# Five places of work in a hybrid decoder layer: row sums' low parts, first halves' transposes, one residual, the last pair's window parts and one token quarter's load

## The chip, the cores and the metric

The kernel runs on one core of one Trainium2 chip. Its time is the device time of one execution in microseconds (us). The core has five engines with a program of their own each: TensorE (PE, matrix products and transposes), VectorE (DVE), ScalarE (ACT), GpSimd (POOL) and SyncE (SP, which here only starts DMA transfers, as POOL and ACT also do). Each engine takes its instructions in order, so an instruction that waits holds up all that stand behind it on its engine. PE's loads of the stationary operand have rows of their own (PEld).

## What is computed

One step of a layer with three head groups, for 4096 prompt tokens and 64 sample tokens, in fp32 with a model width of 1024:

```
h = rmsnorm(x, g_pre);  z = h @ w_in                       # 1024 -> 10 column groups
conv, gate:   out_a = silu(cg) * cb * conv3(cc * ch)       # 256 channels
window:       out_b = silu(ag) * window_attention(q, k, v) # 8 heads of 64, 2 kv heads, window 128, a sink per head
memory:       out_c = silu(mg) * memory_attention(mq)      # 4 heads, 256 memory tokens
y = concat(out_a, out_b, out_c) @ w_out                    # 1024 -> 1024
x = x + rmsnorm(y, g_post)
```

Outputs are the new x of both token groups, and the last keys, values and convolution inputs.

## The kernel before

**Numbers.** Operands of PE are pairs of fp32r parts: a high part `hi` (a cast on ACT, line 358, or 1676 in the pairs) and a low part `lo`, the difference, on DVE (line 359, or 1679). A product is three matmuls: hi x hi, lo x hi, hi x lo.

**Input projection.** It runs in three phases of the output columns (`ph` 0, 1, 2; the first is phase one in the change's title). The 4160 tokens form eight blocks of 520, and each block's product with the weights is a Strassen-Winograd form of seven products `p` over halves of tokens, inputs and columns, so that the tokens of a block are quarters: B11 and B12, B21 and B22. `T1` to `T4` (`x_5T`, `hi_5T`, ...) are differences of quarters. A quarter is loaded to a tile of its own (`x_6B`: a quarter of block 6) or into the shared tiles `place`, scaled on ACT (line 326), and split (358, 359). In the first phase, `next_block` (line 545) says at which product of a block the quarters of the next one are loaded, by SP's queue, and scaled. In the same phase the token rows `nat` are loaded for the norms' sums of squares (ACT line 276), and in blocks 3 to 6 four weight tiles `ws..A` are loaded and summed on DVE (lines 201 to 207) for later phases. The products are PE line 368.

**Attention and output projection.** 4096 tokens are sixteen chunks of 256, each with two halves `h` (odd and even). A half goes through three steps, called between product steps of the output projection: `first_half` (window scores `ws`, the products of the half before, gates, window softmax), `memory_half` (memory scores `xs`) and `second_half`, where `window_turns` transposes the softmaxed window scores `sm` on PE (line 1376, `wt`); ACT copies them (1305, `wpt`), POOL masks them into `wpv` and `wpt` (1310, 1313), and PE reads these in line 1388. For the memory heads, DVE takes the maximum (`xmx`, `xnm`), ACT the exponentials (1178, `xp`), DVE reciprocals of the sums (`xrd`, 1184), POOL scales (1190), PE transposes (1366, `xt`), and ACT copies (1367).

**Output projection.** Its first three chunk pairs are six plain blocks of 128 tokens (`Block.run`, line 1618: two column halves p of eight steps k); a block ends with a norm: DVE `yn` (1645), ACT squares (1646), POOL `yst` (1653), and a residual `xr` (DVE 1658, with its store), which `finish_block` takes from the list `left` at step (0, 5) of the next block. Between them sit the weight sums `wsum..`, `wt..` (1836 to 1848) that the pairs need. From chunk 3 on, `Pair.run` (line 1686) computes two blocks at once in a seven-product form, whose operands are `pa` (plain parts), `pr` (row sums), `pw` (window parts), `pd` (diagonal sum) and `pc` (column differences), and whose accumulators are `y_c`. There are thirty positions `e` in a pair; a table says which piece of another step is called at which position.

**What sets the order.** PE's order is the order of the code. In the first phase the other engines also run in written order; in attention, the other engines' order is set by a scheduler from priorities and dependences, except where `keep_in_program_order` pins it. So the positions of the table move instructions of all engines. These are the lines:

```python
memory_at = {...} | turn_of(16, 27)
second_at = {h: n + (12 if h == 2 else 9 if h == 8 else 8) for h, n in first_at.items()} | turn_of(18, 32)
...
at(e - 10, p.plain_parts)
at(e - 3, p.row_sums)
...
at(e + 4, lambda p=p: p.window_parts(0))
at(e + 7, lambda p=p: p.window_parts(1))
```

Of the kernel before, what the change touches and what calls it, by code (L numbers as in the profile page):

```python
# [52 lines left out]
def hybrid_layer(ctx: ExitStack, tc: tile.TileContext, a: dict):  # L53
# [491 lines left out]
    def next_block(ph, b, p):  # L545
# [5 lines left out]
        if nph < 2:  # L551
            jobs += {0: "B11", 3: "B21 B12", 4: "B22"} .get(p, "").split() if ph == 0 else \
                    {0: "B11", 3: "B21", 4: "B12", 5: "B22"}.get(p, "").split()
            jobs = [load(o) for o in jobs]
# [1024 lines left out]
    class Block:  # L1579
# [38 lines left out]
        def run(self, starts):  # L1618
# [5 lines left out]
            for p in range(2):  # L1624
                cs = slice(512 * p, 512 * p + 512)
                acc = psum("z", f"y{b}_{p}")
                for k in range(KT):
                    starts.get((p, k), lambda: None)()
                    if m < P:
                        l, w = self.terms[p][k]  # L1630
                        for r in range(2):
                            TE.matmul(acc, l, w[:, r], start=k + r == 0, stop=k + r == KT)
                        continue
                    if (p, k) == (0, 5):
                        finish_block()
                    for i, (l, r) in enumerate(((0, 0), (1, 0), (0, 1))):
                        TE.matmul(acc, self.hl[l][:, k], wo[k][p][:, r], start=k + i == 0, stop=k + i == KT + 1)  # L1637
# [25 lines left out]
    class Pair:  # L1663
# [24 lines left out]
        def sums_of(self, raw, t, *terms):  # L1688
# [5 lines left out]
            return lambda pinned=False: self.lows(t, raw, pinned)  # L1694

        def row_sums(self):
            t = self.parts("pr")
            self.rows = [t[:, :, 0:2], t[:, :, 2:4]]
            raw = sums["sum"].tile([P, 512], F32, tag="sum", name=f"sum{self.c}")
            self.sums_of(raw, t, *((self.mix(slice(2, 4), n), self.mix(slice(0, 2), n), ALU.add) for n in range(2)))()  # L1700

# [19 lines left out]
        def run(self, starts, sample=lambda: None):  # L1721
# [70 lines left out]
            if not last:  # L1792
# [3 lines left out]
                product(c22, self.w[1], plain(1, range(4, 8)), False)  # L1796
                added(1, 1, c22)
                scaled(1, 1)
                ends(1)
# [122 lines left out]
    memory_at = {h: n + (7 if h == 2 else 3 if h == 8 else 3) for h, n in first_at.items()} | turn_of(16, 27)  # L1922
    second_at = {h: n + (12 if h == 2 else 9 if h == 8 else 8) for h, n in first_at.items()} | turn_of(18, 32)
    first_at |= turn_of(12, 24)

    what, pending = {}, []
    between = []

# [19 lines left out]
    for c, p in pairs.items():  # L1948
# [7 lines left out]
        at(e + 6, lambda: left.pop(0)(True) if left else None)  # L1956
        at(e + 7, lambda p=p: p.window_parts(1))
        at(e + (7 if c == NCH - 1 else 9), p.diagonal_sum)
# [151 lines left out]
```

## Time and profile before

| | |
|---|---|
| time, median of 3 runs | 1528.67 us (1528.08 to 1529.4) |
| profiled execution, its own time | 1541.16 us |
| its span | 1539.4 us |
| mean granted TensorE clock | 0.996 |
| TensorE, VectorE, ScalarE, GpSimd busy | 98%, 78%, 55%, 25% |
| data moved by DMA | 319.71 MB, mean 208 GB/s |

The span counts from the first to the last instruction of the profiled execution. A row of the timeline reads: start in us, duration in us, engine, line, operation, output <- inputs, sizes, count, and in brackets how long the engine stood idle before it and for whom. Rows that follow one another with the same line and operation are joined. The table of waits gives, for each instruction and the one that it waited for, total us, number and longest. The granted clock in a window is a share of full speed.

### The profile page before, as it was taken

What the parts mean: (1) busy time and instruction counts of PE and PEld (TensorE: products, weight loads), DVE (VectorE), ACT (ScalarE), POOL (GpSimd) and SP (SyncE); (2) the same over time, 40 slices, a digit from 0 to 9 for tenths busy, and PEclk for the clock granted to TensorE, in tenths of its full rate; (3) what the DMA queues carried; (4) which work ended last, traced back from release to release, by engine and by line L of the source; (5) the groups of instructions that cost most, each with busy time, mean ns of one, the idle gap of its engine ahead of it and who ended that gap; (6) DMA issues with size and microseconds to landing.
All of it is one profiled execution on the core that took longest, in us unless ns stands there. A gap on an engine that the chain in (4) does not pass through costs nothing.

```text
span 1539.4 us, 30947 instructions
## 1 busy us (share of the span) xinstructions
PE 1510.8 (98%) x11497; PEld 1386.8 (90%) x11497; DVE 1208.1 (78%) x2089; ACT 843.1 (55%) x2066; POOL 391.5 (25%) x576
## 2 busy tenths in 40 slices
PE   9999999999999999999999999999999999999997
PEld 9999999999999999999999999777788778777875
DVE  6779876899988777896777768876877888888864
ACT  6676655565422222354454536665666666666652
POOL 0222322211300000000111301234455444454631
PEclk9999999999999999999999999999999999999999
DMA  9989999878855333478787698998755555666552
GB/s 261 170 241 217 285 288 260 244 255 290 223 182 180 114 123 125 165 234 288 225 269 239 208 305 246 282 234 222 200 165 155 158 165 160 172 172 165 152 196 69
DMA packets 217322, 319.71 MB, mean 208 GB/s; under 512 B 37397, under 2 KB 143381, under 8 KB 217141
## 3 DMA queue, kind: packets, MB, share of 16 engines
q1 hardware_dynamic: 196837, 273.54, 60.5%
q0 software_dynamic: 19616, 43.15, 10.5%
q8 instruction: 91, 1.49, 0.4%
q10 hardware_dynamic: 720, 1.05, 0.2%
q14 instruction: 58, 0.48, 0.1%
HBM read 208.50 MB, written 110.15 MB: 207 GB/s over the span
## 4 chain that ended last, share of the span: by engine, by line
PE 68%; DVE 12%; issue 4%; DMA 4%; ACT 3%; POOL 1%; SPq 1%; DVEq 0%; ACTq 0%; POOLq 0%
PE c L368 49%; PE y_c L1737 9%; PE y L1637 2%; DVE sm L1295 2%; DVE sm L1341 1%; PE xt L1366 1%; DVE xr L1658 1%; DMA kst<-qd 1%; PE ws L1331 1%; DVE xmx L1169 1%; ACT sm L1287 1%; DMA nat<-in_x_p 1%; DVE wmx L1279 1%; PE mem_acc L790 1%; DMA zs<-in_w_out 1%
## 5 line engine op out<-in xcount | busy, mean ns | idle before, releaser
L375 DVE TENSOR_TENSOR z<-c,z 128x520 f32<-128x520 f32 (+1 forms) x308 | 194.3, 644 | 82.2 <-PE c L368 81.3
L1737 PE MATMUL y_c<-wo,pw 128*128 128x512 f32 (+1 forms) x636 | 158.4, 391 | 0.5 <-DVE yn L1775 0.5
L1287 ACT ACTIVATE sm<-sm,wnm 128x128 f32<-128x128 f32 x256 | 99.4, 389 | 72.0 <-DVE wnm L1281 72.0
L1737 PEld LDWEIGHTS y_c<-wo,pw 128*128 128x128 f32 x636 | 114.1, 188 | 27.2 <-issue 5.4
L1190 POOL TENSOR_SCALAR xp<-xp,xrd 128x256 f32<-128x256 f32 x128 | 67.6, 548 | 80.0 <-DVE xrd L1184 75.5
L1178 ACT ACTIVATE xp<-xs,xnm 128x256 f32<-128x256 f32 x128 | 59.0, 473 | 24.6 <-DVE xnm L1170 24.1
L737 POOL CAST wmask<-negs 128x256 uint8<-128x256 f32 x1 | 1.2, 1213 | 270.0 <-DMA negs<-in_wmask 270.0
L1313 POOL TENSOR_SCALAR_AFFINE_SELECT wpt<-wpt 128x512 f32<-128x512 f32 x64 | 59.0, 934 | 39.8 <-ACT wpt L1305 37.9
L1310 POOL TENSOR_SCALAR_AFFINE_SELECT wpv<-wpt 128x512 f32<-128x512 f32 x62 | 51.8, 848 | 58.5 <-ACT wpt L1305 58.4
L1637 PE MATMUL y<-wo,mh 128*128 128x512 f32 x192 | 64.5, 398 | 0.2 <-ACT y L1646 0.2
L276 ACT ACTIVATE nat<-nat 104x1024 f32<-104x1024 f32 x40 | 42.3, 1057 | 35.2 <-DMA nat<-in_x_p 35.2
L1331 PE MATMUL ws<-kst,q 128*128 128x256 f32 (+1 forms) x480 | 55.7, 297 | 0.0
L1341 DVE COPY_PREDICATED sm<-wmask,ws 128x512 f32<-128x512 uint8 x60 | 40.5, 729 | 18.5 <-ACT sm L1340 18.5
L1658 DVE SCALAR_TENSOR_TENSOR xr<-yn,yst,xr 128x1024 f32<-128x1024 f32 (+2 forms) x35 | 52.4, 1501 | 3.1 <-POOL yst L1653 3.0
L407 ACT CAST zh<-z 128x520 fp32r<-128x520 f32 x56 | 33.3, 624 | 36.5 <-DVE z L375 31.9
L377 ACT COPY z<-c 128x520 f32<-128x520 f32 (+1 forms) x44 | 24.4, 554 | 51.2 <-PE c L368 47.0
L1331 PEld LDWEIGHTS ws<-kst,q 128*128 128x128 f32 (+1 forms) x480 | 46.4, 187 | 4.1
L1287 ACT ACTIVATION_READ_ACCUMULATOR sm<-sm,wnm 128x1 f32 x256 | 47.9, 187 | 0.0
L1295 DVE TENSOR_TENSOR sm<-sm,wrd 128x512 f32<-128x512 f32 x64 | 44.8, 700 | 1.1
L164 POOL DMA_DIRECT2D md<-th x48 | 26.3, 548 | 75.6 <-DVE th L425 61.3
L1367 ACT COPY xp<-xt 128x1024 f32<-128x1024 f32 x30 | 30.4, 1014 | 27.1 <-POOL wpv L1310 16.1
L1737 PE MATMUL y_c<-wtT,pa 128*128 128x512 f32 x156 | 41.1, 400 | 3.8 <-DVE yn L1755 3.8
(1035 smaller groups left out, 5563.5 us busy)
## 6 DMA issues: line engine op xcount, KB each, us to landing
q<-qd SPq DMA_DIRECT2D x168, 128.0 KB
xr<-in_x_p SPq DMA_DIRECT2D x32, 512.0 KB
nat<-in_x_p SPq DMA_DIRECT2D x39, 416.0 KB
o_yp<-xr SPq DMA_DIRECT2D x31, 512.0 KB
kst<-qd SPq DMA_DIRECT2D x112, 128.0 KB
md<-th POOLq DMA_DIRECT2D x48, 260.0 KB, 7.3
qd<-zh SPq DMA_DIRECT2D x48, 260.0 KB
qd<-z SPq DMA_DIRECT2D x48, 260.0 KB
```

Of the source, the lines that this page charges most:

```text
L368: TE.matmul(bank[:, :HW], l, r, start=first and i == 0, stop=last and i == 3 * KH - 1)
L375: add = lambda dst, other: V.tensor_tensor(dst, c, other, op=ALU.add)
L1178: S.activation(p[:, i, :], s[:, i, :], AF.Exp, bias=nm[:, i : i + 1], scale=SCALE, accum_out=den[:, i : i + 1])
L1190: G.tensor_scalar(p[:, i, :], p[:, i, :], self.rds[h][:, i : i + 1], 0.5, op0=ALU.mult, op1=ALU.mult)
L1287: S.activation(sm[:, hh, :], sm[:, hh, :], AF.Exp, bias=nm[:, hh : hh + 1], scale=SCALE, accum_out=den[:, hh : hh + 1])
L1295: V.tensor_tensor(sm, sm, rd.unsqueeze(2).to_broadcast([P, 4, P]), op=ALU.mult)
L1313: G.affine_select(p3, p3, pattern=[[0, 4], [1, P]], compare_op=ALU.is_ge, fill=0.0, base=0, channel_multiplier=-1)
L1331: TE.matmul(out(kvh, col, bank), q(kvh, col, bank)[r], k(kvh, part)[r], start=first, stop=True, skip_group_check=not first, **place)
L1341: V.copy_predicated(sm4, third["wmask"].unsqueeze(1).to_broadcast([P, 2, 2, P]), s4[:, :, :, 0:P])
L1637: TE.matmul(acc, self.hl[l][:, k], wo[k][p][:, r], start=k + i == 0, stop=k + i == KT + 1)
L1658: x = V.scalar_tensor_tensor(self.xr[:m, cs], yn[:m, cs], st[:m, 3:4], self.xr[:m, cs], op0=ALU.mult, op1=ALU.add)
L1737: TE.matmul(acc, a[:, l, k], w[:, r, cs], start=first, stop=k == len(ws) - 1 and i == 2, skip_group_check=not new)
```

## The change

It adds and removes no operation on data; it changes where five pieces stand.

1. `next_block`: in the first phase B12 of the next block is loaded at product 2, no longer with B21 at product 3.
2. `Block.run`: block 5 does not call `finish_block` at step (0, 5). Block 4's residual stays on the list until the next call, which stands in the first half that follows. Its store moves with it on SP, behind two more loads of weights.
3. `row_sums`: from chunk 4 on only the sums and the cast are issued at position e - 3. The low part (`row_lows`) is put on a list, `behind`, that `Pair.run` empties behind the second block's `yn` (line 1755).
4. `second_at`: odd halves' second half at position 19 and not 18 of a pair.
5. The last pair calls `window_parts(1)` at e + 5 and not e + 7.

```diff
-            jobs += {0: "B11", 3: "B21 B12", 4: "B22"} .get(p, "").split() if ph == 0 else \
+            jobs += {0: "B11", 2: "B12", 3: "B21", 4: "B22"}.get(p, "").split() if ph == 0 else \
...
-                    if (p, k) == (0, 5):
+                    if (p, k) == (0, 5) and b < 2 * PLAIN_PAIRS - 1:
                         finish_block()
...
+        def row_lows(self, t, raw):
+            raw = raw.rearrange("p (b n) -> p b n", n=P)
+            tc.keep_in_program_order(V.tensor_tensor(t[:, 1], raw, f(t[:, 0]), op=ALU.subtract))
+
         def row_sums(self):
...
-            self.sums_of(raw, t, *((self.mix(slice(2, 4), n), self.mix(slice(0, 2), n), ALU.add) for n in range(2)))()
+            parts = self.sums_of(raw, t, *((self.mix(slice(2, 4), n), self.mix(slice(0, 2), n), ALU.add) for n in range(2)))
+            if self.c == PLAIN_PAIRS:
+                parts()
+            else:
+                S.copy(t[:, 0], raw.rearrange("p (b n) -> p b n", n=P))
+                behind.append(lambda: self.row_lows(t, raw))
...
                 added(1, 1, c22)
+                while behind:
+                    behind.pop(0)()
                 scaled(1, 1)
...
-    second_at = {h: n + (12 if h == 2 else 9 if h == 8 else 8) for h, n in first_at.items()} | turn_of(18, 32)
+    second_at = {h: n + (12 if h == 2 else 9 if h == 8 else 8) for h, n in first_at.items()} | turn_of(19, 32)
...
-    between = []
+    between, behind = [], []
...
-        at(e + 7, lambda p=p: p.window_parts(1))
+        at(e + (5 if c == NCH - 1 else 7), lambda p=p: p.window_parts(1))
```

How instructions move, at three places. First SP's queue in block 5 of the first phase, from the row broadcast `rb` to the next rows `nat`: `ws4A` are the four weight tiles, `x_6B` is B21 and `place` (in two pieces) B12 of block 6. Before, and then with the change:

```order
L251 DMA rb_3193<-rowd_81 128x520
L201 DMA ws4A_3222<-in_w_in 128x512
L201 DMA ws4A_3224<-in_w_in 128x512
L201 DMA ws4A_3226<-in_w_in 128x512
L201 DMA ws4A_3228<-in_w_in 128x512
L265 DMA nat_3247<-in_x_p 104x1024
L238 DMA x_6B_3262<-in_xt 128x4x260
L238 DMA place<-in_xt 128x4x12
L238 DMA place<-in_xt 128x4x248
```

```order
L251 DMA rb_3193<-rowd_81 128x520
L238 DMA place<-in_xt 128x4x12
L238 DMA place<-in_xt 128x4x248
L201 DMA ws4A_3224<-in_w_in 128x512
L201 DMA ws4A_3226<-in_w_in 128x512
L201 DMA ws4A_3228<-in_w_in 128x512
L201 DMA ws4A_3230<-in_w_in 128x512
L265 DMA nat_3249<-in_x_p 104x1024
L238 DMA x_6B_3264<-in_xt 128x4x260
```

B12's two transfers stand ahead of the weights, one `nat` and B21 now, where they stood behind them.

Second, DVE in plain block 5, from a weight sum to the first half behind it: `xr` is block 4's residual, `wtT` the low part of the weight sum, `yn` the block's own, `wes`, `wden` and `wrd` belong to the window softmax of the next half. One piece of the difference, and the other:

```order
L1652 TENSOR_SCALAR yst_13021<-yst_13021 128x1
L1842 TENSOR_TENSOR wsumT_13078<-wsumT_13078,zs 128x512
L1658 SCALAR_TENSOR_TENSOR xr_12455<-yn_13020,yst_13021,xr_12455 128x1024
L1848 TENSOR_TENSOR wtT_13300<-wsumT_13078,wtT_13300 128x512
L1645 TENSOR_TENSOR yn_13288<-y_0_13290,gpost 128x512
L1341 COPY_PREDICATED sm_0_13412<-wmask,ws_0_13375 128x512
```

```order
L1283 TENSOR_TENSOR wes_0_13420<-wnm_0_13418,sink 128x4
L1253 TENSOR_TENSOR mix_13000<-mix_13000,wo_1_13391 128x2x4x64
L1405 TENSOR_TENSOR mix_13000<-mix_13000,wo_1_13391 128x2x128
L1283 TENSOR_TENSOR wes_1_13432<-wnm_1_13430,sink 128x4
L1658 SCALAR_TENSOR_TENSOR xr_12455<-yn_13020,yst_13021,xr_12455 128x1024
L1292 TENSOR_TENSOR wden_0_13423<-wden_0_13423,wes_0_13420 128x4
L1294 RECIPROCAL wrd_0_13443<-wden_0_13423 128x4
L1295 TENSOR_TENSOR sm_0_13410<-sm_0_13410,wrd_0_13443 128x512
```

The residual stood ahead of `wtT` and `yn`; it stands behind the second `wes` and ahead of the softmax's sums now.

Third, a pair, on two engines. At the end of its run, DVE (`sm`: window softmax of a half; `pr`: the low part of the next pair's row sums; `yn` of line 1755, 1764 in the changed file), before and with the change:

```order
L1295 TENSOR_TENSOR sm_1_13876<-sm_1_13876,wrd_1_13912 128x512
L1679 TENSOR_TENSOR pr_13958<-sum_13959,pr_13958 128x512
L1184 RECIPROCAL xrd_0_13950<-xden_0_13944 128x2
L1755 TENSOR_TENSOR yn_1_13517<-y_c_13823,s_3_13520 128x512
L1184 RECIPROCAL xrd_1_13954<-xden_1_13947 128x2
```

```order
L1295 TENSOR_TENSOR sm_1_13876<-sm_1_13876,wrd_1_13912 128x512
L1764 TENSOR_TENSOR yn_1_13517<-y_c_13823,s_3_13520 128x512
L1184 RECIPROCAL xrd_0_13950<-xden_0_13944 128x2
L1698 TENSOR_TENSOR pr_13958<-sum_13959,pr_13958 128x512
L1184 RECIPROCAL xrd_1_13954<-xden_1_13947 128x2
```

`pr` goes behind `yn` and the first reciprocal. In the pair's odd half, POOL (the masks `wpv`, `wpt` and the memory heads' `xp`), before and with the change:

```order
L1310 AFFINE_SELECT wpv_0_13777<-wpt_0_13775 128x512
L1313 AFFINE_SELECT wpt_0_13775<-wpt_0_13775 128x512
L1190 TENSOR_SCALAR xp_1_13744<-xp_1_13744,xrd_2_13751 128x256 x2
L1190 TENSOR_SCALAR xp_1_13744<-xp_1_13744,xrd_3_13755 128x256 x2
L1310 AFFINE_SELECT wpv_1_13782<-wpt_1_13780 128x512
L1313 AFFINE_SELECT wpt_1_13780<-wpt_1_13780 128x512
```

```order
L1190 TENSOR_SCALAR xp_1_13744<-xp_1_13744,xrd_2_13751 128x256 x2
L1190 TENSOR_SCALAR xp_1_13744<-xp_1_13744,xrd_3_13755 128x256 x2
L1310 AFFINE_SELECT wpv_0_13780<-wpt_0_13778 128x512
L1310 AFFINE_SELECT wpv_1_13785<-wpt_1_13783 128x512
L1313 AFFINE_SELECT wpt_0_13778<-wpt_0_13778 128x512
L1313 AFFINE_SELECT wpt_1_13783<-wpt_1_13783 128x512
```

The first window head pair's masks stood ahead of the scaling of `xp`; all four masks stand behind it now.

## The prediction

> **What bounds the kernel now.** I read the page's first part, then the table of what TensorE (PE) waits for, because only a wait of the engine that sets the end can be won back, and then windows and the timeline around each wait that the change touches.
>
> ```profile
> span 1539.4 us, 30947 instructions
> PE 1510.8 (98%) x11497; PEld 1386.8 (90%) x11497; DVE 1208.1 (78%) x2089; ACT 843.1 (55%) x2066; POOL 391.5 (25%) x576
> ...
> PE y_c L1737 <- DVE yn L1755: 3.8, 11, 0.6
> PE wt L1376 <- DVE sm L1295: 2.1, 11, 0.4
> PE c L368 <- ACT hi_6B L358: 1.8, 1, 1.8
> PE wo L1388 <- ACT xp L1367: 1.7, 1, 1.7
> PE c L368 <- DVE lo_6B L359: 0.9, 1, 0.9
> PE y_c L1737 <- ACT yn L1746: 0.8, 1, 0.8
> ```
>
> PE is busy for 1510.8 of 1539.4 us, so all idle time together is 28.6 us, and the change removes and adds no arithmetic: it can only win from these 28.6 us or add to them. The columns of the waits are total us, count and longest. The six rows hold 11.1 us and name the places that the diff touches: the first two come once in each of eleven pairs, the others once.
>
> A long wait also costs clock behind it. Windows of PE alone (start:end, length, busy, granted clock, DMA share, GB/s):
>
> ```profile
> 270.00:275.00 5.00, 5.00 (x32) 0.68 1.21 99
> ...
> 1045.00:1050.00 5.00, 3.33 (x27) 0.80 0.99 338
> 1050.00:1055.00 5.00, 5.00 (x37) 0.86 0.84 280
> ```
>
> The first stands behind the 1.8 + 0.9 us waits, the other two around the 1.7 us wait. The lost clock is 0.32 x 5 = 1.6 us in the one, (0.20 + 0.14) x 5 = 1.7 us in the other. Behind the single 0.8 us wait there is none.
>
> **The change part by part.** *1. The row sums' low part behind the residual's first half (11 pairs).* DVE runs `pr` and then `yn`, and PE waits for `yn`.
>
> ```profile
> 1202.74 0.69 DVE L1679 TENSOR_TENSOR pr<-sum,pr 128x512 fp32r<-128x512 f32 x1
> 1203.42 0.67 DVE L1755 TENSOR_TENSOR yn<-y_c,s 128x512 f32<-128x512 f32 x1
> 1204.15 1.66 PE L1737 MATMUL y_c<-wtT,pa 128*128 128x512 f32 x6 [0.32 <-DVE yn L1755]
> 1204.76 0.57 ACT L1770 COPY s<-y_c 128x512 f32<-128x512 f32 x1
> 1205.64 2.89 PE L1737 MATMUL y_c<-wo,pr 128*128 128x512 f32 x12
> 1207.46 0.68 DVE L1775 TENSOR_TENSOR yn<-s,y_c 128x512 f32<-128x512 f32 x1
> 1208.37 2.90 PE L1737 MATMUL y_c<-wo,pw 128*128 128x512 f32 x12
> ```
>
> With `yn` ahead of `pr`, `yn` ends up to 0.69 us sooner and the 3.8 us of the row go. But PE then meets the next two: the copy at 1204.76 ends at 1205.33, and PE's product behind it starts 0.31 later; L1775 ends at 1208.14, and PE starts 0.23 later. PE's start at 1204.15 is 0.06 behind the end of `yn` (1204.09), so 0.06 to 0.14 of such a distance is delivery, and 0.09 to 0.17 is all that PE can come forward at the second one; the chain up to L1775 holds no `pr`. `pr` itself moves to about 1203.5 to 1204.2 and is wanted at 1205.64, so its delay is covered by 1.4 us. Of the two small reciprocals for which POOL's `xp` waits, both stood behind `pr`; the first now comes ahead of it, the second stays behind. I take 0.09 x 11 = **-1.0**; bounds 0 and -3.8.
>
> *2. The first halves' transposes one product step later (11 pairs).*
>
> ```profile
> 1221.38 0.60 PE L1376 MATMUL wt<-ident,sm 128*128 128x128 f32 x4
> 1222.13 0.63 PE L1376 MATMUL wt<-ident,sm 128*128 128x128 f32 x4 [0.15 <-DVE sm L1295]
> 1222.50 0.16 DVE L1170 TENSOR_SCALAR xnm<-xmx 128x2 f32<-128x2 f32 x1
> 1226.70 1.03 PE L1366 MATMUL xt<-ident,xp 128*128 128x128 f32 x8
> 1229.28 0.43 PE L1388 MATMUL wo<-wpv,vt 64*64 64x256 f32 x2
> ...
> 1473.37 0.47 ACT L1178 ACTIVATE xp<-xs,xnm 128x256 f32<-128x256 f32 x1
> ...
> 1478.31 1.22 POOL L1313 TENSOR_SCALAR_AFFINE_SELECT wpt<-wpt 128x512 f32<-128x512 f32 x2
> ```
>
> Eight transposes without a wait take 1.03 us (`xt`); the eight of `wt` take 1222.76 - 1221.38 = 1.38, so 0.35 is lost per pair, 3.8 us in all. Three products y_c<-wo,pc (0.7 us) ahead of them cover that. But ACT's copy of `wt` now comes behind the four exponentials, and POOL scales `xp` before it masks `wpv` and `wpt`, so PE's read at 1229.28 hangs on a new order. Pair 15 runs this very order before the change: from its first exponential (1473.37) to POOL's last mask (1478.31 + 1.22 = 1479.53) it takes 6.16 us. Here the exponentials can start when `xnm` ends, 1222.66, so the masks end at 1228.8 to 1229.0 and PE can read at about 1228.9 to 1229.15, where it would like 1228.93. A gain of 0.13 to 0.35; I take 0.22 x 11 = **-2.4**. Bounds: -3.8, and, if exponentials and masks each come 0.4 late, +2.
>
> *3. Block 4's residual out of the way of the last plain block.*
>
> ```profile
> 1042.79 1.64 DVE L1658 SCALAR_TENSOR_TENSOR xr<-yn,yst,xr 128x1024 f32<-128x1024 f32 x1 [0.90 <-POOL yst L1653]
> 1044.31 1.86 PE L1331 MATMUL ws<-kst,q 128*128 128x256 f32 x16
> 1044.36 1.12 DVE L1848 TENSOR_TENSOR wtT<-wsumT,wtT 128x512 fp32r<-128x512 f32 x1
> 1044.88 1.67 POOL L1313 TENSOR_SCALAR_AFFINE_SELECT wpt<-wpt 128x512 f32<-128x512 f32 x2
> 1045.39 0.68 DVE L1645 TENSOR_TENSOR yn<-y,gpost 128x512 f32<-128x512 f32 x1
> 1046.69 1.00 ACT L1367 COPY xp<-xt 128x1024 f32<-128x1024 f32 x1
> ...
> 1052.07 0.69 DVE L1253 TENSOR_TENSOR mix<-mix,wo 128x512 f32<-128x512 f32 x1 [1.10 <-PE wo L1059]
> ```
>
> DVE stood 0.90 for POOL's `yst` and then spent 1.64 on `xr`; `wtT`, `yn` and through ACT the copy that PE waited 1.7 us for came behind. Without it that copy ends between 1047.69 - 2.54 = 1045.15 and 1047.69 - 1.64 = 1046.05, and PE is through with `ws` at 1046.17. What is late next is POOL's mask, done at 1046.55: a wait of 0.4 to 0.5 can stay, or none, if POOL is quicker with DVE elsewhere. With 0.3 left, 1.4 of the wait and the 1.7 of clock come back: **-3.1**; bounds -1.1 (clock lost again) and -3.4. At its new place `xr` and its store lie before a DVE wait of 1.10 us (1052.07), which hides most of 1.64; without that cover 0.5 to 1.6 would pass to the masks behind it.
>
> *4. The last pair's window parts two positions earlier.* The casts and the low part leave the place ahead of ACT's `yn` L1746, for which PE waited 0.8 us once: **-0.8**, bounds -0.8 and +0.5 (one cast's length for the sample tokens' softmax behind it).
>
> *5. B12 at the third product.* SP now issues it ahead of the four loads of the weight sums, one `nat` and B21. For phase one's stretch the row of all engines, then SP, DVE, PE and ACT in block 5:
>
> ```profile
> 200.00:300.00 100.00, 96.40 (x791) 95.44 (x790) 78.63 (x96) 54.15 (x94) 27.17 (x46) 0.98 0.94 263
> ...
> 241.57 1.24 DVE L359 TENSOR_TENSOR lo_5T<-place,hi_5T 128x1040 fp32r<-128x1040 f32 x1 [1.21 <-ACT hi_5T L358]
> 242.11 3.60 SPq L201 DMA_DIRECT2D ws4A<-in_w_in  x4
> 247.34 2.68 SPq L238 DMA_DIRECT2D place<-in_xt  x2
> 250.82 0.69 DVE L204 TENSOR_TENSOR ws4S<-ws4A,ws4A 128x512 f32<-128x512 f32 x1 [1.37 <-DMA ws4A<-in_w_in]
> 253.11 1.24 DVE L359 TENSOR_TENSOR lo_5B<-place,hi_5B 128x1040 fp32r<-128x1040 f32 x1
> 254.40 0.39 PE L368 MATMUL c<-lo_5B,w_0S 128*128 128x260 f32 x1
> 262.77 1.72 ACT L326 ACTIVATE place<-place,gpre 128x260 f32<-128x260 f32 x4 [2.38 <-DMA place<-in_xt]
> ```
>
> The transfers fill the engines (share 0.94, 263 GB/s), and DVE already waits 1.37 us for the weights at 250.82. Behind that sum stands `lo_5B`, which ends at 254.35 for a PE that takes it at 254.40: there is 0.05 us of slack. B12 is 128 x 1040 fp32 = 0.53 MB, 2.0 us at 263 GB/s, and this now lies ahead of the weights. SP can issue it only once `lo_5T` has freed the place (242.81), takes 2.68, and so starts the weights at 245.5 instead of 242.11: 3.4 us later, if the issue and not the backlog sets their landing. The same order holds in blocks 3 and 4. Won is the wait of ACT at 262.77 and with it, at most, PE's 1.8 + 0.9 and 1.6 of clock, 4.3; but B21 now lands last, at about the time B12 did, so these shrink mainly because PE itself comes later. Between -4.3 (no new wait) and 3 x 3.4 + 3 x 1.6 - 4.3 = +10.7 I take a stall of 2.0 once and half of it twice, since one stream of data can't be late by the same bytes each time, and one drop of the clock: 2 + 1 + 1 + 1.6 - 4.3 = **+1.3**.
>
> The Trainium skill, "DMA: Bandwidth & Descriptors" (Queues, rings and completion order), says that each DMA engine takes the descriptors of a ring in order: it fits the late weights above, and by it alone the price is the 2.0 us of transfer, not the 3.4 of issue.
>
> *Sum:* -1.0 - 2.4 - 3.1 - 0.8 + 1.3 = -6.0. The profiled execution took 1541.16 us with a span of 1539.4; the runs' median is 1528.67, 12.5 us less. The waits are of order and not of length, so I take the difference over as it is: 1528.7 - 6.0 = **1522.7 us**, the profiled span at about 1533.
>
> **The rivals.** *A, all waits come back*: the row sums' 3.8, the transposes' 3.8, 3.4 in the plain block, 0.8 and 4.3: -16.1, 1512.6. For it: each edit meets its row. Against: the distances of 0.23 and 0.31 us behind part 1 and the 0.05 us in part 5.
>
> *B, the pairs only pass their waits on*: parts 1 and 2 give nothing and part 5 comes out at zero: -3.9, 1524.8. For it: POOL's chain of 6.16 us fits to a tenth or two. Against: PE's 0.35 us stands at the transposes and the slack there is free of POOL.
>
> *C, slower: the weights' loads behind B12.* With a lateness L in each of blocks 3 to 5 and a clock drop each, part 5 costs 3 L + 4.8 - 4.3; with the pairs at nothing the sum is 3 L - 3.4. It decides from L = 2.2 on (+3.1); at 3.4 it is +6.8, 1535.5. For it: 0.05 us of slack, and DVE waiting for these weights already. Against: the backlog in the queue, which hides a late issue.
>
> *D, the clock does not come back.* A drop that falls where a fixed period ends, whatever the length of the gap, would stay after the plain block: -6.0 + 1.7 = -4.3, 1524.4. For it: a drop followed a wait of only 1.7 us. Against: both drops stand behind the longest waits, none elsewhere between 200 and 1500 us among the rows read. The Trainium skill, "TensorE: Matmul & The Clock Gate" (Part 1: The HAM clock gate), has the clock fall after an idle window of about 3.4 us on a free-running period; the trace shows falls behind far shorter gaps, so removing such a gap need not, by that rule, return them.
>
> **How the numbers follow.** My forecast 0.44, A 0.12, B 0.17, D 0.10, C 0.17. The measurement can tell about 0.2% (3.1 us) from no change: faster is below 1525.6, slower above 1531.7. Faster: 0.41 of the forecast, A's 0.12, 0.11 of B and 0.07 of D, 0.71. Slower: most of C, 0.15. The rest, 0.14, is the same. The forecast's own range, from a full plain block and full transposes to pairs at a third and L = 2, is 1518 to 1526; to 8 in 10 it reaches half of A and half of C: 1513 to 1532.
>
> **What would show it.** In the pairs the row `PE y_c L1737 <- DVE yn L1755` gone, with a row for L1770 or L1775 instead; `PE wt <- DVE sm` gone and at most 0.3 us at L1388 for POOL `wpt`. At about 1046 no wait over 0.6 us and windows at clock 1.00. The tail's 0.8 gone. In phase one DVE L204 later by about 2 us against `hi`, with new PE waits for `lo_3B`, `lo_4B`, `lo_5B`. I am wrong if those waits exceed 2.2 us each (C), or if B12 lands early with the weights on time (A); and if pairs lose at L1388 more than 0.35 us each.

## The result and the profile after

| | before | with the change |
|---|---|---|
| median of 21 runs each | 1530.39 us (1526.46 to 1537.87) | 1526.31 us (1521.85 to 1528.75) |
| ratio of the times | | 0.9966, 95% interval 0.9956 to 0.9975 |
| profiled execution, its span | 1539.4 us | 1522.4 us |

The change takes 0.34% or 5.2 us off (3.8 to 6.7 by the interval; 0.0034 x 1530.4); the two medians lie 4.1 us apart. The two profiled spans differ by 17.0 us, and most of that is not the change: the execution profiled before took 1541.16 us, more than the slowest of the 21 timed runs.

The first part of the page of the changed kernel, and PE's waits (total us, count, longest):

```profile
span 1522.4 us, 30940 instructions
PE 1504.4 (99%) x11497; PEld 1382.3 (91%) x11497; DVE 1198.9 (79%) x2089; ACT 842.7 (55%) x2066; POOL 402.2 (26%) x576
...
PE c L368 <- DVE lo_4B L359: 1.0, 1, 1.0
...
PE wt L1376 <- DVE sm L1295: 0.6, 2, 0.4
PE y_c L1746 <- DVE yn L1784: 0.6, 1, 0.6
...
PE y_c L1746 <- ACT y L1646: 0.2, 1, 0.2
```

(Lines behind 1698 have moved by 9 to 11: L1746 is L1737 of before, L1764 L1755, L1779 L1770, L1784 L1775.) Of the six rows shown with the prediction one has a rest, the transposes' (0.6 us, twice and not in every pair); the others are gone. The pairs' own measure is the tile `vtp`, which PE writes once per pair; the view of one tile gives its first and last start over eleven pairs, here before and then after:

```profile
L1912 PE MATMUL vtp<-ident,vT x22: 272/273/273, 1096.0 to 1454.6; 128*128 128x128 f32 x22
```

```profile
L1923 PE MATMUL vtp<-ident,vT x22: 272/273/273, 1083.7 to 1439.0; 128*128 128x128 f32 x22
```

Ten periods take 358.6 us before and 355.3 after: 0.33 us less per pair, though two waits of 0.35 us and more per pair have gone (0.57 and 0.35 by the table under number 3). The rest went into a new wait, which the table of PE's waits does not show, as it is a weight load's (PEld). Timeline of the changed kernel, odd half of a pair, and then the same products before:

```profile
1208.29 1.03 PE L1376 MATMUL wt<-ident,sm 128*128 128x128 f32 x8
...
1209.64 0.47 ACT L1178 ACTIVATE xp<-xs,xnm 128x256 f32<-128x256 f32 x1 [1.25 <-DVE xmx L1169]
...
1211.03 1.85 POOL L1190 TENSOR_SCALAR xp<-xp,xrd 128x256 f32<-128x256 f32 x4 [5.83 <-DVE xrd L1184]
...
1214.47 1.22 POOL L1313 TENSOR_SCALAR_AFFINE_SELECT wpt<-wpt 128x512 f32<-128x512 f32 x2
...
1215.16 0.43 PE L1388 MATMUL wo<-wpv,vt 64*64 64x256 f32 x2
1215.44 0.94 PE L1388 MATMUL wo<-wpt,vt 64*64 64x256 f32 x3
...
1215.74 0.19 PEld L1388 LDWEIGHTS wo<-wpt,vt 64*64 64x64 f32 x2 [0.38 <-POOL wpt L1313]
```

```profile
1229.28 0.43 PE L1388 MATMUL wo<-wpv,vt 64*64 64x256 f32 x2
...
1229.56 0.38 PE L1388 MATMUL wo<-wpt,vt 64*64 64x256 f32 x2
```

The transposes run in 1.03 us, without a wait. POOL's last mask ends at 1215.69, and PE, which began with line 1388 at 1215.16, stands in the middle of it: the products of this line end 1.22 us after they began (1216.38), where they took 0.66 before.

In the plain blocks the chain that the prediction followed reads, after:

```profile
1033.61 0.68 DVE L1645 TENSOR_TENSOR yn<-y,gpost 128x512 f32<-128x512 f32 x1
...
1034.70 1.86 PE L1331 MATMUL ws<-kst,q 128*128 128x256 f32 x16
1034.73 1.22 POOL L1313 TENSOR_SCALAR_AFFINE_SELECT wpt<-wpt 128x512 f32<-128x512 f32 x2
...
1035.03 1.02 ACT L1367 COPY xp<-xt 128x1024 f32<-128x1024 f32 x1
...
1036.49 0.43 PE L1388 MATMUL wo<-wpv,vt 64*64 64x256 f32 x2
```

The copy ends at 1036.05 and POOL's masks at 1035.95, both ahead of PE, which comes from `ws` at 1036.5 and does not wait. The residual is at its new place, ahead of the softmax:

```profile
1040.68 1.28 DVE L1658 SCALAR_TENSOR_TENSOR xr<-yn,yst,xr 128x1024 f32<-128x1024 f32 x1
1041.88 0.70 DVE L1292 TENSOR_TENSOR wden<-wden,wes 128x4 f32<-128x4 f32 x1
```

Windows of PE alone around the two places of the drops of clock before (busy, clock, DMA share, GB/s) show none after:

```profile
265.00:270.00 5.00, 5.00 (x44) 1.00 1.06 88
270.00:275.00 5.00, 5.00 (x44) 1.00 0.68 87
1030.00:1035.00 5.00, 5.00 (x31) 1.00 1.01 218
1035.00:1040.00 5.00, 5.00 (x52) 1.00 0.95 335
```

**Stages of every profiled execution** (us, worked out from the traces: from the start, or from the mark before, to PE's first product of the second phase, of the third, of the plain blocks, of the first pair, of the last pair, and to the end):

| kernel | first phase | second | third | plain blocks | 12 pairs | last pair and tail |
|---|---|---|---|---|---|---|
| before | 350.3 | 322.6 | 267.4 | 117.6 | 429.8 | 51.7 |
| the change | 344.0 | 319.9 | 266.8 | 114.2 | 426.7 | 50.8 |
| b12_only | 350.0 | 320.4 | 267.3 | 117.5 | 429.6 | 52.0 |
| lows_only | 343.4 | 319.7 | 266.9 | 115.9 | 429.6 | 51.6 |
| turn_only | 342.6 | 319.6 | 267.4 | 115.9 | 426.0 | 51.6 |
| plain_only | 347.6 | 322.7 | 267.4 | 114.2 | 430.5 | 51.7 |
| tail_only | 342.1 | 319.1 | 267.0 | 115.9 | 430.0 | 50.1 |
| no_b12 | 350.7 | 319.1 | 267.0 | 114.2 | 426.7 | 50.4 |
| best | 342.7 | 322.6 | 267.4 | 114.2 | 426.8 | 50.1 |
| pool_light | 346.3 | 319.8 | 266.9 | 114.1 | 426.9 | 50.4 |
| xr_out | 342.8 | 322.4 | 267.3 | 114.2 | 429.7 | 50.4 |
| xr_out_light | 344.1 | 319.1 | 267.0 | 114.1 | 430.2 | 50.4 |
| xr_pool2 | 350.3 | 322.6 | 267.4 | 114.2 | 446.1 | 50.5 |
| xr_out_pin | 344.7 | 322.3 | 267.4 | 114.1 | 418.6 | 51.2 |

Two columns follow the code: the pairs, and the plain blocks (117.5 with a drop of clock, 115.9 without one, 114.1 to 114.2 with the residual moved). The tail follows it nearly: 51.6 to 52.0 without its edit, 50.1 to 51.2 with it. Two do not: lows_only, turn_only, plain_only and tail_only have the first two phases of the kernel before, row for row, and in these five executions the first phase takes 342.1 to 350.3, the second 319.1 to 319.7 or 322.6 to 322.7. So a single execution can't tell a first phase from another, and the columns that follow the code carry the verdicts below, with the timed ratios beside them.

### The profile page after: what moved, and what is told of

Its sections match the earlier page's. It is cut to its first block, busy times and chain, and to the rows that moved or that the text cites. A ratio compares the mean times of both kernels' runs of the same rounds, so it can differ in the third digit from the quotient of the medians.

```text
span 1522.4 us, 30940 instructions
## 1 busy us (share of the span) xinstructions
PE 1504.4 (99%) x11497; PEld 1382.3 (91%) x11497; DVE 1198.9 (79%) x2089; ACT 842.7 (55%) x2066; POOL 402.2 (26%) x576
## 3 DMA queue, kind: packets, MB, share of 16 engines
q8 instruction: 91, 1.49, 0.4%
## 4 chain that ended last, share of the span: by engine, by line
PE 83%; DVE 6%; DMA 5%; issue 2%; ACT 2%; POOL 1%; SPq 0%; DVEq 0%; ACTq 0%; POOLq 0%
PE c L368 49%; PE y_c L1746 16%; PE ws L1331 3%; PE y L1637 2%; PE wo L1394 2%; PE wo L1059 2%; PE xt L1366 2%; PE xs L1353 2%; PE wt L1376 1%; PE wo L1388 1%; DMA md<-th 1%; DVE z L375 1%; PE mem_acc L790 1%; DMA zs<-in_w_out 1%; DMA ws2A<-in_w_in 1%
## 5 line engine op out<-in xcount | busy, mean ns | idle before, releaser
L1746 PE MATMUL y_c<-wo,pw 128*128 128x512 f32 (+1 forms) x636 | 158.7, 391 | 0.6 <-DVE yn L1784 0.6
L1746 PEld LDWEIGHTS y_c<-wo,pw 128*128 128x128 f32 x636 | 114.0, 188 | 27.6 <-issue 5.7
L1190 POOL TENSOR_SCALAR xp<-xp,xrd 128x256 f32<-128x256 f32 x128 | 71.8, 577 | 196.4 <-DVE xrd L1184 191.8
L1310 POOL TENSOR_SCALAR_AFFINE_SELECT wpv<-wpt 128x512 f32<-128x512 f32 x62 | 56.9, 938 | 8.7 <-ACT wpt L1305 8.6
L1313 POOL TENSOR_SCALAR_AFFINE_SELECT wpt<-wpt 128x512 f32<-128x512 f32 x64 | 46.3, 742 | 38.7 <-ACT wpt L1305 38.2
L1658 DVE SCALAR_TENSOR_TENSOR xr<-yn,yst,xr 128x1024 f32<-128x1024 f32 (+2 forms) x35 | 50.8, 1454 | 3.3 <-POOL yst L1653 2.8
L1746 PE MATMUL y_c<-wo,pc 128*128 128x512 f32 (+1 forms) x162 | 45.2, 400 | 0.0
L1637 PEld LDWEIGHTS y<-wo,mh 128*128 128x128 f32 x192 | 36.1, 188 | 8.9 <-issue 1.0
```

The source lines that it names most:

```text
L1190: G.tensor_scalar(p[:, i, :], p[:, i, :], self.rds[h][:, i : i + 1], 0.5, op0=ALU.mult, op1=ALU.mult)
L1310: G.affine_select(pv.rearrange("p (h q) -> p h q", h=4), p3, pattern=[[0, 4], [-1, P]], compare_op=ALU.is_gt, fill=0.0, base=0, channel_mu ...
L1313: G.affine_select(p3, p3, pattern=[[0, 4], [1, P]], compare_op=ALU.is_ge, fill=0.0, base=0, channel_multiplier=-1)
L1658: x = V.scalar_tensor_tensor(self.xr[:m, cs], yn[:m, cs], st[:m, 3:4], self.xr[:m, cs], op0=ALU.mult, op1=ALU.add)
L1746: TE.matmul(acc, a[:, l, k], w[:, r, cs], start=first, stop=k == len(ws) - 1 and i == 2, skip_group_check=not new)
```

## The experiments

**1. B12 alone (b12_only).**

```diff
-            jobs += {0: "B11", 3: "B21 B12", 4: "B22"} .get(p, "").split() if ph == 0 else \
+            jobs += {0: "B11", 2: "B12", 3: "B21", 4: "B22"}.get(p, "").split() if ph == 0 else \
```

> Only the load of B12 is moved (to product 2 of the first phase); the rest is the kernel before. Theory, from the two traces: the waits for lo_2B (two), lo_4T, hi_6B and lo_6B go, one for lo_4B of about 1 us comes, and with the wait of 1.8 + 0.9 us goes the drop of clock behind it: 4 to 6 us less up to the end of the first phase, ratio 0.996 to 0.998. Rival, the forecast's step: the weights land later in blocks 3 to 5 and each stalls PE, a sum of -1 to +3 us, ratio 0.9995 to 1.002, with DVE L204 about 2 us later against the products in all three blocks.

Ratio 1.0004 (0.9990 to 1.0018; 12 runs, 1532.63 us): no difference that can be told. Of PE's waits in it, these two, and one of 0.5 us for `lo_3B`, stand at the place that the forecast named:

```profile
PE c L368 <- DVE lo_4B L359: 1.3, 1, 1.3
PE c L368 <- DVE lo_5B L359: 1.0, 1, 1.0
```

The theory of 4 to 6 us from the two first traces falls. Over all fourteen executions of the table the seven with the early load (the change, b12_only, pool_light and the four with xr) end the first phase at 346.0 us on average, the seven without it at 345.6. A wait for `lo_5B`, behind the weights, stands in all seven of the one kind (0.2 to 1.7 us by PE's starts) and in two of the other; waits for `lo_4T`, `lo_5T` and `hi_6B` stand mainly where B12 is late; the seven with the early load have four of them, of 0.2 to 0.75 us. DVE's first sum of weights (L204), counted from PE's first product with one of the block's differences `T`, starts 0.8, 1.1 and 0.8 us later in blocks 3, 4 and 5 on the average of the seven, where the prediction had about 2. The edit changes which transfer is late, and by these fourteen executions not how late the stage is.

**2. The row sums alone (lows_only).** The diff is that of `row_lows`, `row_sums` and `behind`.

```diff
-            self.sums_of(raw, t, ...)()
+            S.copy(t[:, 0], raw.rearrange("p (b n) -> p b n", n=P))
+            behind.append(lambda: self.row_lows(t, raw))
```

> Only the row sums' low part is moved behind yn. Theory, from the trace of the changed kernel: the whole 0.5 us per pair comes back, since the copies and sums behind (L1770, L1775) follow PE and come forward with it: a pair's period falls by 0.45 to 0.55 us, 5 to 6 us in all, ratio 0.996 to 0.997. Rival, the forecast's step: the next two waits hold PE after 0.09 us per pair, 1 us in all, ratio 0.999 to 1.000.

In the trace a pair takes what it took before (429.6 against 429.8 for twelve), and tile `vtp` says the same, 358.3 for ten:

```profile
L1923 PE MATMUL vtp<-ident,vT x22: 272/273/273, 1084.1 to 1442.4; 128*128 128x128 f32 x22
```

The wait for `yn` is gone, and PE's weight loads wait for the next two instead, ACT's copy and DVE's sum behind it:

```profile
1084.62 0.64 ACT L1749 ACTIVATE s<-yn 128x512 f32<-128x512 f32 x1
...
1085.23 0.59 ACT L1779 COPY s<-y_c 128x512 f32<-128x512 f32 x1
...
1085.87 1.23 PEld L1746 LDWEIGHTS y_c<-wo,pr 128*128 128x128 f32 x6 [0.48 <-ACT s L1779]
...
1087.32 1.23 PEld L1746 LDWEIGHTS y_c<-wo,pr 128*128 128x128 f32 x6 [0.22 <-DVE s L1781]
```

ACT has no idle time between its exponentials, which begin at 1082.81, and this copy. So the forecast's step holds and the theory falls. The timed ratio does not agree: 0.9978 (0.9964 to 0.9992; 9 runs). Nothing in the pairs' stage carries 3 us; the first two phases vary by more than that from execution to execution, which may be it, but that was not settled. Beside the other edits there is no gain: numbers 6 and 7 differ by this edit alone, and their medians are 1525.5 us without it and 1525.44 with it.

**3. The transposes alone (turn_only).**

```diff
-    second_at = {h: n + (12 if h == 2 else 9 if h == 8 else 8) for h, n in first_at.items()} | turn_of(18, 32)
+    second_at = {h: n + (12 if h == 2 else 9 if h == 8 else 8) for h, n in first_at.items()} | turn_of(19, 32)
```

> Only the odd halves' transposes are put one product step later. Theory, from the trace of the changed kernel: the wait of 0.35 us at the transposes goes, but POOL's last mask ends later than PE's read at L1388 and holds it by about 0.55 us, so a pair's period grows by 0.1 to 0.25 us, 1 to 2.8 us in all, ratio 1.0005 to 1.002. Rival, the forecast's step: the masks are ready in time and 0.2 us per pair are won, 2.4 us in all, ratio 0.998 to 0.999.

Ratio 0.9973 (0.9958 to 0.9987; 12 runs, 1526.77 us), and the twelve pairs fall from 429.8 to 426.0 us; ten periods of `vtp` take 355.1:

```profile
L1912 PE MATMUL vtp<-ident,vT x22: 272/273/273, 1083.8 to 1438.9; 128*128 128x128 f32 x22
```

The theory of a loss falls: this edit alone has all that the pairs gain in the traces. Where PE's time goes within a pair, as distances between the starts of its pieces (medians over five pairs, worked out from the traces, us; the pieces that are not listed are equal to 0.03):

| piece of PE | before | lows_only | turn_only | the change | pool_light | xr_out_pin |
|---|---|---|---|---|---|---|
| even half's wt, at the pair's end | 0.88 | 0.87 | 0.87 | 0.87 | 0.99 | 0.87 |
| vtp | 0.71 | 0.14 | 0.25 | 0.14 | 0.14 | 0.14 |
| y_c<-wtT,pa | 1.49 | 1.76 | 1.49 | 1.47 | 1.76 | 1.47 |
| y_c<-wo,pr | 2.72 | 2.93 | 2.72 | 2.79 | 2.95 | 2.73 |
| y_c<-wo,pw | 2.76 | 2.82 | 2.76 | 2.77 | 2.80 | 2.72 |
| odd half's wt | 1.14 | 1.18 | 0.79 | 0.79 | 0.79 | 0.79 |
| wo, line 1388, of the odd half | 0.59 | 0.59 | 1.06 | 1.18 | 0.59 | 0.59 |
| whole pair | 35.78 | 35.79 | 35.45 | 35.50 | 35.54 | 34.83 |

In turn_only the wait at line 1388 is there (+0.47), as the theory had it, but the wait at `vtp` has shrunk as well (-0.46), though nothing was done to it, and the 0.35 at the transposes is the pair's gain. The even half's window scores `ws` stand between the two: the transposes ahead of them, line 1388 behind. A wait ahead of `ws` delays the row of DVE and ACT work that starts with the scores and ends at the pair's end, where PE waits for it; a wait behind `ws` only uses up the time that PE would wait there anyway. The table fits this but does not show it; numbers 8 to 12 test it.

In this execution PE also waited 1.70 us in the plain block, as before, and the clock did not drop (PE's timeline, then windows of PE):

```profile
1037.15 0.43 PE L1388 MATMUL wo<-wpv,vt 64*64 64x256 f32 x2 [1.70 <-ACT xp L1367]
```

```profile
1034.00:1039.00 5.00, 3.31 (x39) 1.00 0.91 283
1039.00:1044.00 5.00, 5.00 (x37) 1.00 1.01 339
```

**4. The plain block alone (plain_only).**

```diff
-                    if (p, k) == (0, 5):
+                    if (p, k) == (0, 5) and b < 2 * PLAIN_PAIRS - 1:
```

> Only block 4's residual is moved out of plain block 5. Theory and forecast agree on the wait of 1.7 us: it goes. They part on the clock: if the drop to half clock behind it came from this wait, it goes in this profile as well, -3 us, ratio 0.998; if it comes at fixed times whatever the gaps, a drop of 3.4 us length is seen somewhere in most profiles and the kernel wins 1.4 us, ratio 0.999.

Ratio 0.9982 (0.9963 to 1.0001; 12 runs, 1530.1 us): the times alone can't tell it from no difference. The stage takes 114.2 us. Without the edit it takes 115.9 where no drop falls into it (three executions) and 117.5 where one does (two). So the wait is worth 1.7 us in every execution, and the other 1.7 of the two first traces is a drop that comes in some. None of the nine executions with the residual moved has a drop in the plain blocks. Drops elsewhere stay: this execution has one of 3.41 us at 62 us, behind another wait.

**5. Tail alone (tail_only).**

```diff
-        at(e + 7, lambda p=p: p.window_parts(1))
+        at(e + (5 if c == NCH - 1 else 7), lambda p=p: p.window_parts(1))
```

> Only the last pair's window parts are called two positions earlier. Theory and forecast: the wait of 0.8 us for ACT's yn goes and the stretch behind the last pair's start falls from 51.7 to about 50.8 us; nothing else changes, ratio 0.999 to 1.000. Rival: the softmax of the sample tokens comes later by a cast and the stretch stays at 51.5 us or more.

The stretch falls from 51.7 to 50.1 us. Ratio 1.0002 (0.9988 to 1.0016; 12 runs, 1530.3 us): 1.6 us less is 0.999, inside the interval, and can't be told from nothing by the times. Why the stretch falls by more than the 0.8 us of the wait is not shown.

**6. Without the row sums' edit and B12 (best).** `before` with edits 2, 4 and 5 of the list.

> Three of the five edits: the transposes one product step later, block 4's residual behind, the last pair's window parts earlier; row sums and B12 as in the kernel before. Theory: the row sums' move gives nothing alone and costs 0.05 us per pair beside the later transposes, so a pair's period is 35.44 us, the four stages from the pairs on are the shortest of all, and the ratio is 0.9945 to 0.9965, not above that of the change. Rival: the row sums' move and the transposes' add up, so the period without it is 35.6 or more and the ratio 0.997 to 0.998.

Ratio 0.9961 (0.9945 to 0.9978; 12 runs, 1525.5 us); twelve pairs 426.8 against 426.7 with the row sums moved. Neither of the two edits that are left out adds anything that can be seen; the kernel is as fast as the whole change, not clearly faster.

**7. Without B12 (no_b12).** The change with the diff of number 1 undone.

> The changed kernel with B12 loaded at product 3 again. Theory, from the profile with B12 alone: the early load makes waits for lo_3B, lo_4B and lo_5B of 1 to 3 us in all and saves as much or less elsewhere, so without it the first phase ends as early or up to 2 us earlier, and the ratio to the kernel before is that of the change or lower, 0.995 to 0.997. Rival, from the first two traces: the early load is worth 4 us and more, so the ratio is 0.998 to 0.9995.

Ratio 0.9964 (0.9946 to 0.9982; 12 runs, 1525.44 us): as the change's 0.9966. The rival of 4 us falls.

**8. POOL's chain shortened (pool_light).** On top of the change:

```diff
-                G.tensor_scalar(p[:, i, :], p[:, i, :], self.rds[h][:, i : i + 1], 0.5, op0=ALU.mult, op1=ALU.mult)
+                (V if h == 3 and self.c > PLAIN_PAIRS else G).tensor_scalar(...)
```

> The changed kernel with two of the four scalings of xp in each odd half (from chunk 4 on) on DVE and not on POOL, the same arithmetic. Theory: POOL's masks then end 0.9 us earlier and PE's wait of 0.56 us at L1388 goes; what is won there is lost at the pair's end, where ACT's copy L1779 and DVE's L1784 stand close behind PE, so the period stays at 35.3 to 35.5 us and the ratio to the kernel before is that of the change. Rival: POOL's masks alone bind the pair, the period falls to 34.9 to 35.0 and 5 to 6 us are won, ratio 0.992 to 0.994.

Line 1388 falls from 1.18 to 0.59, and the pieces at the pair's end grow by 0.12 + 0.29 + 0.16 + 0.03 = 0.60: the period is 35.54 after 35.50. Ratio 0.9976 (0.9962 to 0.9990; 12 runs, 1526.79 us). The wait was moved and not removed, as the theory said. Its timeline shows what the pair's end waits for. From the first row shown to `pr` DVE has no gap, and among these instructions stands the residual of the pair's first block (the two scalings stand ahead of the scores, at 1214.09):

```profile
1218.25 1.36 DVE L1341 COPY_PREDICATED sm<-wmask,ws 128x512 f32<-128x512 uint8 x2 [0.26 <-ACT sm L1340]
...
1221.81 0.23 DVE L1283 TENSOR_TENSOR wes<-wnm,sink 128x4 f32<-128x4 f32 x2
1221.95 1.83 DVE L1658 SCALAR_TENSOR_TENSOR xr<-yn,yst,xr 128x1024 f32<-128x1024 f32 x1
```

**9 and 10. DVE's row shortened, without and with POOL's (xr_out, xr_out_light).** The residual of each pair's first block is left out, on the change and on number 8.

```diff
-                x = V.scalar_tensor_tensor(self.xr[:m, cs], yn[:m, cs], st[:m, 3:4], self.xr[:m, cs], op0=ALU.mult, op1=ALU.add)
+                x = None if out else V.scalar_tensor_tensor(...)     # out: n == 0 and c < NCH - 2
```

> The changed kernel without the residual's multiply-add (DVE L1658, 1.6 to 1.8 us) for the first block of each pair up to chunk 13; what is stored for those blocks is the input alone. Theory: two things hold a pair at 35.5 us, and both must go: POOL's masks at L1388 (0.56 us) and DVE's unbroken row of work from the window scores to the pair's end. With the row shortened alone the wait at L1388 stays, and the period stays at 35.3 to 35.5. Rival: the row of DVE alone sets the period, which falls to 34.9 to 35.1.

> The same work left out, and two of the four scalings of xp in each odd half on DVE. Theory: with both gone, the period falls to 34.9 to 35.1, the length of PE's own work. Rival: PE or another chain holds at 35.4 whatever is taken from DVE.

Both periods are 35.77 us, longer than with the work in: neither theory nor rival. In number 10 the waits that number 8 has at `wt` and `pa` go (0.97 to 0.87 and 1.76 to 1.47), but the piece ahead of `pw` grows from 2.95 to 3.59. In number 9 it grows from 2.79 to 3.07, and the wait at line 1388 stays. Timeline of xr_out_light:

```profile
1229.34 0.88 DVE L1679 TENSOR_TENSOR pd<-diag,pd 128x256 fp32r<-128x256 f32 x1 [0.40 <-ACT pd L1676]
1230.15 0.67 DVE L1784 TENSOR_TENSOR yn<-s,y_c 128x512 f32<-128x512 f32 x1
...
1230.97 1.85 PE L1746 MATMUL y_c<-wo,pw 128*128 128x512 f32 x7 [0.69 <-DVE yn L1784]
```

The scheduler of DVE's order, which had the residual no more, put `pd` ahead of the `yn` that PE waits for. The experiment had changed two things.

**11. The same work on POOL (xr_pool2).** On number 8, nothing left out:

```diff
+                if pool:
+                    G.tensor_scalar(yn[:m, cs], yn[:m, cs], st[:m, 3:4], 1.0, op0=ALU.mult, op1=ALU.mult)
+                    x = G.tensor_tensor(self.xr[:m, cs], yn[:m, cs], self.xr[:m, cs], op=ALU.add)
```

> The changed kernel with two of the four scalings of xp in each odd half on DVE, and the residual of each pair's first block (to chunk 13) on POOL, as a scaling and an addition: the same arithmetic, nothing left out. Theory: POOL is idle there for 2.4 and 4.9 us, DVE's row is 1.8 us shorter, and the period falls to 34.9 to 35.2: 3 to 6 us less than the change, ratio to the kernel before 0.992 to 0.995. Rival: POOL's scaling and addition (4 us and more by the rows of 128x512) slow DVE at the same time, as xnm was slowed from 0.20 to 0.60 us beside a mask, or come too late for the row sums behind them; the period stays at 35.4 or grows, ratio 0.996 or more.

The rival holds: ratio 1.0088 (1.0072 to 1.0103; 7 runs, 1545.41 us), period 37.3 us. `pd` is ahead of `yn` here too, and DVE is held while POOL adds:

```profile
1123.46 2.43 POOL L1660 TENSOR_TENSOR xr<-yn,xr 128x1024 f32<-128x1024 f32 x1
...
1124.36 2.25 DVE L1283 TENSOR_TENSOR wes<-wnm,sink 128x4 f32<-128x4 f32 x2
...
1125.85 0.74 POOL L1697 TENSOR_TENSOR sum<-mix 128x256 f32<-128x256 f32 x1
```

The two instructions that take 0.23 us in number 8 take 2.25: the first ends at 1125.91, 0.02 us behind POOL's addition, and the second at 1126.61, 0.02 us behind POOL's next. ACT's exponentials and the sums wait behind them.

**12. Number 10 with DVE's order kept (xr_out_pin).**

```diff
-            self.sums_of(sums["sum"].tile(...), self.diagonal, (...))()
+            tc.keep_in_program_order(self.sums_of(sums["sum"].tile(...), self.diagonal, (...))(True))
```

> The same work left out as in the run before the last (the residual's multiply-add of each pair's first block, to chunk 13), two of the four scalings of xp in each odd half on DVE, and the diagonal sum's cast and low part pinned, so that DVE's order is that of the kernel with the scalings on DVE, but for the missing instruction. In the run without the pin the scheduler put pd ahead of L1784 and made a wait of 0.87 us per pair. Theory: with POOL's wait and DVE's row both shortened and no such wait, the period falls to 34.9 to 35.1 us. Rival: L1784 or ACT still holds PE and the period stays at 35.4 or more.

The period is 34.83 us; ten periods of `vtp` take 348.5, and no piece of PE in the table has a wait left:

```profile
L1923 PE MATMUL vtp<-ident,vT x22: 272/273/273, 1086.1 to 1434.6; 128*128 128x128 f32 x22
```

So after the change two things hold a pair at 35.5, POOL's masks and DVE's row, and with both taken away it runs at 34.8, with no wait of PE left in the table's pieces. That the masks alone would hold it once DVE's row is shorter is not shown: in number 9, which tested this, DVE's order changed too, and it was not run with the order kept. No run here reaches 34.8 with the residual kept.

## Why the prediction came out

The forecast was 1522.7 us from a median of 1528.67, that is -6.0 or 0.39%; measured were -5.2, or 0.34% (0.25 to 0.44). It holds, but the sum came nearer than its terms, and that is luck in part: the row sums and the clock were put too high, the transposes and the tail too low, and a loss of 5.6 us from B12's stalls was set against a gain of 4.3 from waits of one execution, neither of which the kernel shows at that size.

*Row sums, -1.0.* The step was right in kind: the next waits hold PE. It was still too high: 0.09 us per pair was reckoned, and the trace of the edit alone has 0.00 (35.79 after 35.78), though its timed ratio is left unexplained. What I had not seen is that ACT's copy hangs on ACT's own row, which starts with the exponentials, and not on PE's product or on `yn`.

*Transposes, -2.4.* The sign was right, the size too small (-3.8 us over twelve pairs, alone), and the working wrong. It failed in the sentence "Here the exponentials can start when `xnm` ends": they start at 1209.64 in the changed kernel, when the second maximum (L1169) has ended, 0.7 us behind the end of `xnm` at 1208.95, and POOL's masks are late by 0.5 us. A sign of being wrong that the prediction names has come, a loss at line 1388 of more than 0.35 us per pair: it is 0.59 (1.18 after 0.59). That this loss cost nothing in the sum of a pair is due to DVE's row, which the prediction did not follow from the even half's scores to the pair's end.

*Plain block, -3.1.* The wait of 1.7 us came back whole, and the 0.3 us left for POOL did not appear: its masks took 1.22 us where they took 1.67. The step that failed is "and the 1.7 of clock come back": the wait stood in five executions without the edit, and the clock dropped in two of them, so that on the average of the five only 0.7 us of clock was to be had. Rival D was right that a fixed period decides (the figures stand in the last section), and wrong that the drop stays whatever the gap: with the wait gone, none of nine executions has it. The Trainium skill, "TensorE: Matmul & The Clock Gate" (Part 1: The HAM clock gate), has a free-running window decide, and the executions agree in that; they do not agree that an idle window of about 3.4 us is needed, since a wait of 1.7 us sufficed.

*Tail, -0.8.* -1.6 by its own trace, -0.9 by the change's; the times can't tell it.

*B12, +1.3.* Measured +0.6 (-1.5 to +2.8) alone. The step was right that the weights behind B12 become late, by about 1 us and not 2: `lo_5B` is waited for in every execution with the edit (in the change's for 0.2 us only). The 4.3 us set against it, from the rows `hi_6B` and `lo_6B`, were one execution's: of the other six that load B12 late none has them. Rival A took the same rows for a gain that the kernel does not have.

*The transfer from the profile to the median.* "I take the difference over as it is" was the weakest sentence: the execution profiled before stood 12.5 us over the median of the runs shown with it, and these were not waits of its order alone. 7 us lay in the first phase (350.3 after a median of 343.4 of the seven that load B12 late), 3 in the second, 1.7 in the plain blocks' drop of clock. Nor can the change win only from PE's 28.6 us of idle time, as the prediction says at its start: PE's busy time itself fell by 6.4 us from one profile to the other, mostly by the two drops of clock (3.4) and the pace of the last section (about 3). The terms taken from the pairs stood in every pair and could be carried over; those from single waits of the first phase could not.

Of rival B it is true that waits are passed on, but by the row sums only, and that part 5 comes out near zero. C did not come: the lateness behind B12 was 0.2 to 1.7 us, below the 2.2 from which it decides, and in one or two blocks; a single execution has it in three, there at 0.7, 1.5 and 1.1.

## What to carry to other kernels

In this kernel a wait of the bounding engine cost what it delayed, not its length: look which work starts at that engine behind the wait, and follow that work to the next place where the engine waits for it. Here a wait ahead of such a start was lost in full (0.35 us per pair), and one behind it was free (0.47). Before a single wait of one profiled execution is counted as a gain, see whether it recurs, in the other rounds of a loop or in a second execution of the same code; and when an experiment leaves an instruction out, compare the whole order, since a scheduler can move others.

## What the runs showed of the hardware

*Two paces at the same clock.* In the second phase, where PE hardly waits (0.7 us at most between 370 and 640 us) and the granted clock is 1.00, the executions fall into two kinds. The same window, before and then after (length, busy, count of matmuls, clock, DMA share, GB/s):

```profile
400.00:500.00 100.00, 100.00 (x835) 1.00 0.65 206
```

```profile
400.00:500.00 100.00, 100.00 (x845) 1.00 0.59 204
```

Over 370 to 640 us a matmul of 128x260 follows the one before after 120.0 ns in the one kind (before, plain_only, best, xr_out, xr_pool2, xr_out_pin) and after 118.7 in the other eight, on the same code of this phase; it makes most of the 3 us between 322.3 to 322.7 and 319.1 to 320.4. What decides it was not found.

*Drops of clock.* Behind the same wait of 1.6 to 1.7 us in the plain block the clock fell to half for 3.41 us in two executions and not in three. All changes of the clock in an execution lie on one grid of 3.413 us: the two drops of the kernel before start 778.24 us apart, 228 x 3.4133, and those of b12_only 955.73, 280 x 3.4133. In these five executions the place of the wait on this grid separates the two cases. It lies within one period in before (1046.17 to 1047.84 in 1044.57 to 1047.98) and in b12_only (1043.51 to 1045.17 in 1042.23 to 1045.64), and the drop starts when that period ends; in lows_only, turn_only and tail_only a period ends inside the wait, and none comes. How much idle time a period needs is not settled: one in the first phase with 1.8 us had no drop behind it (xr_pool2), one with two waits of 1.5 us in sum had (no_b12).

*DVE beside POOL.* Two additions of 128x4 took 2.25 us and not 0.23 beside POOL's additions of 128x1024 and 128x256, and each ended 0.02 us behind one of these. The Trainium skill, "SBUF — State Buffer" (Who interferes with whom), says that a DVE instruction with two inputs in SBUF contends with a GpSimd instruction that reads SBUF, and that the port pair they share is an exclusive lock; the rows agree.
